# State pass, chunk scan, linear recurrence and gate projections: from a scheduled program to one hand-ordered list of 512 steps

## The chip, the core and the metric

The kernel runs on one core of a Trainium2 chip. The metric is the device time of one execution in microseconds (us). Three runs were timed, and one more execution was profiled; every row below comes from that one.

## What is computed

One layer of a backbone with a context prefix: three token mixers run in parallel on the modulated input, their outputs are gated and merged, then comes a mixture of experts. What matters here lies between the input projections and the merge.

```python
# Mamba-2 branch: chunks of 128 tokens, both directions d, heads in 4 groups
cb = jnp.einsum('bcqgn,bcsgn->bgcqs', cm, bm)
lmat = jnp.exp(_segsum(a))
y_diag = jnp.einsum('bgjcqs,bcsgjp->bcqgjp', cb[:, :, None] * lmat, xs)
st = jnp.einsum('bcsgn,bcsgjp->bcgjpn', bm, xs * decay_in[..., None])   # states
y_off = jnp.einsum('bcqgn,bcgjpn->bcqgjp', cm, entering) * decay_out[..., None]
y = y * jax.nn.silu(z)                                                  # then RMS norm, m2_w_out
# RG-LRU branch: two block projections, then a linear scan in each direction
r = sigmoid(xb @ lru_w_a + b);  ig = sigmoid(xb @ lru_w_x + b)
a_t = exp(-LRU_C * r * softplus(-lru_lam))
v = sqrt(max(-expm1(2.0 * log_a), EPS)) * (ig * xc32)
hd, fin = _linear_scan(a_t, v, h0)
# merge
g = sigmoid(gates)                                                      # 3 x 1024 columns of h @ w_in
merged = g0 * ya + g1 * yb + g2 * yc;  mx = merged @ w_o
x = x + mod_x[2] * mx     # mod = silu(c) @ w_mod + b_mod; mod_x[2] to mod_x[5] are first used after the merge
```

There are 1024 tokens and 256 context tokens, 1024 model columns, 16 heads in 4 groups, 10 chunks (8 of them with outputs), 512 recurrence columns.

## The kernel before, in words

**Precision.** A product of two fp32 matrices is made of three matmuls on rounded halves (high by high, high by low, low by high), 128x128 weights against 512 columns each: L265, L266 and L267 in mm3. ACT makes the high half of a weight block (L127) and VectorE (DVE) the low half (L128).

**The stage changed.** Between the input projections (pool p1) and the merge (pool p3b) stands pool p2. A scheduler orders its instructions on each engine, from their order in the program and their priorities. Its parts are:
- a head: softplus of dt, running sums of the log decay by three matmuls, and their rows, which go through device memory as rowsd (4 groups, 2 directions, 4 heads, 1024 tokens).
- states(): nine steps k with two directions each. An input block xk of 512 KB is loaded, GpSimd (POOL) scales it (L750, xd), PE makes four matmuls (L752, st), DVE carries the running state (L756, L762) and it is written back.
- chunk(g, c): 32 times. The decay rows arrive as rowb, broadcast to 128 partitions (L791); ACT takes the exponential of them (L796, dec); PE makes C*B (L798, pcb); DVE subtracts and bounds in eight instructions (L801); ACT takes the exponential (L802); GpSimd adds the directions (L803); DVE multiplies by pcb (L804); GpSimd scales dec (L805); PE makes eight matmuls into yps (L814, L815). After every fourth chunk come the gating by z and the sum of squares (L824 to L830).
- lru_tile(t): four times two directions. PE makes three lps products of three matmuls for each of two projections (L878), ACT makes tanh, exponentials and a root, DVE makes three element-wise instructions on 1283 columns (L885, L887, L888) and two scans (L890 to L895).
- z_task and gate_task: eight and 24 weight blocks, each 2 x 8 x 3 matmuls. Their matmuls (pj_z, pj_gt) are what PE can do while the chains above wait.
- mod_task(half): twice sixteen blocks of w_mod, 512 KB each, as moving operands of fp32 matmuls with one weight column (L912, pm); rows go to device memory as modd.

**The merge.** For each of eight blocks d of 128 columns, PE makes the products of the S5 and recurrence branches (bov, bog, bol), DVE merges them with the loaded gates, and the Mamba-2 output is scaled and split for the output product (L985, L994, tile ym). SyncE (SP) issues all large loads and stores in one queue, in program order.

In the rows, a matmul that isn't on rounded halves is shown as two records, so the four matmuls of a state product read x8. PEld is the loading of weights, which lies beside PE's matmuls.

## Time and profile before

| what | value |
|---|---|
| median of three runs | 2121.89 us (2120.39 to 2122.43) |
| profiled execution, its own time | 2120.92 us |
| its span, first to last instruction | 2119.14 us |
| mean granted TensorE clock, share of full | 0.956 |
| PE busy over the span | 1919.3 us (91%) |
| DVE busy | 1525.2 us (72%) |
| ACT busy | 1020.3 us (48%) |
| POOL busy | 510.4 us (24%) |
| state and scan stage (p2), by the trace | 523.5 to 1130 us |
| merge of the S5 and recurrence branches | 1130 to 1264 us |

The time of the profiled execution is 1.8 us above its span, which is what lies around the first and the last instruction. Busy shares are means over stages that are bound by different things, so the stage's own rows must be read.

### The profile page before, as it was taken

The numbers are of one execution on the slowest core, as the hardware profiler recorded it, in microseconds if no ns is written. First come the engines' busy times: TensorE is split into PE (matmuls) and PEld (weight loads), VectorE is DVE, ScalarE is ACT, GpSimd is POOL, SyncE is SP. The second block draws the span as 40 slices with busy tenths as digits, with TensorE's granted clock in tenths as the row PEclk, the third lists the DMA queues.
The fourth block names the chain that finished last, engine by engine and source line by source line (L and its number), as shares of the span: only waits on it lengthen the run. The fifth ranks groups of instructions, "written<-read, shape, count | busy, mean of one in ns | idle before, by whom it ended". The sixth has DMA issues, their size and how long they took to land.

```text
span 2119.1 us, 27213 instructions
## 1 busy us (share of the span) xinstructions
PE 1919.3 (91%) x9630; PEld 1516.2 (72%) x9630; DVE 1525.2 (72%) x2232; ACT 1020.3 (48%) x1313; POOL 510.4 (24%) x489
## 2 busy tenths in 40 slices
PE   5989999988889988879999999898299999999997
PEld 2678888877657666456577888687188888888885
DVE  4787788783454777667434655628899999999998
ACT  4434434432213665446332212222188888888785
POOL 1353333330142344233100000234501111100122
PEclk9999999999999999989999999999599999999999
DMA  8234334422586676777666554554599999999983
GB/s 313 54 81 114 101 95 117 122 90 90 180 261 192 186 212 175 242 180 210 208 174 188 180 160 153 186 200 149 196 339 381 400 389 404 387 389 393 391 312 137
DMA packets 301554, 462.67 MB, mean 218 GB/s; under 512 B 39945, under 2 KB 200121, under 8 KB 300393
## 3 DMA queue, kind: packets, MB, share of 16 engines
q1 hardware_dynamic: 297096, 445.19, 62.2%
q0 software_dynamic: 4320, 15.73, 2.9%
q8 instruction: 76, 1.25, 0.2%
q14 instruction: 62, 0.50, 0.1%
HBM read 384.44 MB, written 78.51 MB: 218 GB/s over the span
## 4 chain that ended last, share of the span: by engine, by line
PE 55%; DMA 9%; DVE 7%; issue 2%; ACT 1%; SPq 1%; POOL 1%; DVEq 0%; ACTq 0%; POOLq 0%
PE h_w L1443 6%; PE h_w L1445 6%; PE h_w L1444 6%; PE wo L1268 3%; DMA rowb<-rowsd 3%; PE py_w L1445 3%; PE py_w L1443 3%; PE py_w L1444 3%; PE pj_gt L267 2%; PE pj_gt L265 2%; PE pj_gt L266 2%; DMA wm<-in_w_mod_dram 2%; PE bom L266 1%; PE bom L265 1%; PE st L752 1%
## 5 line engine op out<-in xcount | busy, mean ns | idle before, releaser
L1338 DVE TENSOR_TENSOR el_w<-er_w,eh_w 128x1024 fp32r<-128x1024 f32 x384 | 460.7, 1220 | 25.0 <-ACT eh_w L1337 11.1
L1337 ACT CAST eh_w<-er_w 128x1024 fp32r<-128x1024 f32 x384 | 403.7, 1052 | 135.4 <-PE h_w L1444 58.9
L1443 PE MATMUL h_w<-eh_w,thi_x 128*128 128x512 f32 x512 | 202.9, 396 | 0.0
L1445 PE MATMUL h_w<-el_w,thi_x 128*128 128x512 f32 x512 | 200.2, 391 | 0.0
L1444 PE MATMUL h_w<-eh_w,tlo_x 128*128 128x512 f32 x512 | 199.8, 390 | 0.0
L801 DVE SCALAR_TENSOR_TENSOR rowb<-rowb,XL,lim 128x128 f32<-128x128 f32 x256 | 116.1, 518 | 72.1 <-ACT dec L796 72.1
L265 PE MATMUL pj_gt<-hxh,whi_gt 128*128 128x512 f32 x384 | 155.9, 406 | 11.9 <-ACT gz L779 11.9
L267 PE MATMUL pj_gt<-hxh,wlo_gt 128*128 128x512 f32 x384 | 155.3, 404 | 0.0
L266 PE MATMUL pj_gt<-hxl,whi_gt 128*128 128x512 f32 x384 | 155.1, 404 | 0.0
L1445 PEld LDWEIGHTS h_w<-el_w,thi_x 128*128 128x128 f32 x512 | 96.2, 188 | 20.4
L1444 PEld LDWEIGHTS h_w<-eh_w,tlo_x 128*128 128x128 f32 x512 | 96.5, 188 | 19.6 <-DVE tlo_x L1362 0.4
L1443 PEld LDWEIGHTS h_w<-eh_w,thi_x 128*128 128x128 f32 x512 | 96.5, 188 | 19.2 <-ACT thi_x L1361 0.2
L265 PEld LDWEIGHTS pj_gt<-hxh,whi_gt 128*128 128x128 f32 x384 | 74.4, 194 | 38.0 <-ACT gz L779 16.1
L1346 POOL DMA_INDIRECT xs<-h2d,idx x16 | 23.3, 1459 | 309.5 <-PE tb_x L1354 294.4
L1443 PE MATMUL py_w<-eh_w,thi_h 128*128 128x512 f32 x240 | 96.3, 401 | 0.0
L1445 PE MATMUL py_w<-el_w,thi_h 128*128 128x512 f32 x240 | 94.0, 392 | 0.0
L1444 PE MATMUL py_w<-eh_w,tlo_h 128*128 128x512 f32 x240 | 93.5, 390 | 0.0
L267 PEld LDWEIGHTS pj_gt<-hxh,wlo_gt 128*128 128x128 f32 x384 | 74.4, 194 | 25.4 <-issue 9.6
L266 PEld LDWEIGHTS pj_gt<-hxl,whi_gt 128*128 128x128 f32 x384 | 74.4, 194 | 20.5 <-issue 4.9
L796 ACT ACTIVATE dec<-rowb 64x512 f32<-64x512 f32 x64 | 40.2, 629 | 82.7 <-DMA rowb<-rowsd 72.7
L267 PE MATMUL pj_xb<-hxh,wlo_xb 128*128 128x512 f32 x192 | 76.8, 400 | 0.5 <-DVE wlo_xb L128 0.5
L265 PE MATMUL pj_xb<-hxh,whi_xb 128*128 128x512 f32 x192 | 76.7, 399 | 0.0
(653 smaller groups left out, 4894.7 us busy)
## 6 DMA issues: line engine op xcount, KB each, us to landing
er_w<-in_moe_w_dram SPq DMA_DIRECT2D x384, 512.0 KB
...
```

The source lines that it names most:

```text
L265: T.matmul(ps, wh(k), xh(k), start=(first and k == 0), stop=False)
L266: T.matmul(ps, wh(k), xl(k), start=False, stop=False)
L267: T.matmul(ps, wl(k), xh(k), start=False, stop=(last and k == nk - 1))
L796: A.activation(dec[64 * d:64 * d + 64], rowb[64 * d:64 * d + 64, d], AF.Exp)
L801: V.scalar_tensor_tensor(rowb[:, d, h], rowb[:, d, h], XL[:, c, d, 4 * g + h:4 * g + h + 1], lim[:, d], op0=ALU.subtract, op1=ALU.min)
L1268: T.matmul(st4[i]["ps"][n], ms[i][a][:, k], wo[k][b][:, sl], start=(k == 0 and q == 0), stop=(k == KC - 1 and q == 2))
L1337: A.copy(a, raw)
L1338: V.tensor_sub(b, raw, a.bitcast(F32))
L1346: G.indirect_dma_start(out=xsb[e], out_offset=None, in_=h2d[:, :], in_offset=bass.IndirectOffsetOnAxis(ap=idx[:, e:e + 1], axis=0))
L1443: T.matmul(ps[n], xa[:, j, :], a[:, sl], start=(j == 0), stop=False)
L1444: T.matmul(ps[n], xb[:, j, :], a[:, sl], start=False, stop=False)
L1445: T.matmul(ps[n], xa[:, j, :], b[:, sl], start=False, stop=(j == KC - 1))
```

## The change

The stage is written out as one list of 512 steps under a manual order for DVE, ACT and PE: weight block w (32 of them: eight of z, 24 of gates), column half c and contraction block k. Each step makes the three matmuls of one gate block (L1091 of the new program). All other work is hung on steps by plan(step, function): states from step 22 with 5 steps for each k, chunks from step 54 with 12.4 steps each, recurrence rounds from step 81 with 45 steps for each direction. At one step the planned functions run first, then the gate matmuls, and each engine executes its own instructions in that order. SP is not in the manual order.

GpSimd's element-wise work in the stage (L750, L803, L805, L830 and the recurrence splits L860, L865) moves to DVE. The eight L801 become two instructions on 128x1024. rowsd is laid out by chunk, so the broadcast load reads 4 KB in one piece for each partition instead of eight of 512 bytes. The buffers of rowb, xe and bc go from three to four, and xk borrows two more. The stage has a PSUM pool of its own, with two banks each for gates, pcb, yps (shared with st) and lps. The softplus of dt and the constants of the recurrence move to the end of p1. The modulation leaves PE and the stage: the merge loads the same 32 blocks of w_mod, multiplies and adds them on DVE (four and 28 instructions on 128x1024), and sums over partitions with eight matmuls; the tiles of ym share 16 buffers with these blocks.

```diff
+ST0, STP = 22, 5
+CH0, CHP = 54, 12.4
+LR0, LRP = 81, 45
+MEN3 = {mybir.EngineType.DVE, mybir.EngineType.Activation, mybir.EngineType.PE}
...
+            if hb == 7:
+                softplus(dt, 320, p1, "d")
+                lru_consts()
...
-    rowsd = dr.tile([4, 2, 4, S], F32, name="rowsd")
+    rowsd = dr.tile([4, 8, 2, 4, P], F32, name="rowsd")
...
+    ps2 = tc.alloc_tile_pool(name="ps2", bufs=1, space=PSUM, reuse_waits="tile")
+    pb2 = lambda tag, nm: ps2.tile([P, 512], F32, tag=tag, name=nm, bufs=2)
+    with tc.tile_pool(name="p2", bufs=1, reuse_waits="tile") as p2, tc.manual_schedule(engines=MEN3):
+
+        steps = [(w, c, k) for w in range(32) for c in range(2) for k in range(KC)]
...
+        def plan(at, f, *args):
+            todo.setdefault(max(int(at), 0), []).append((f, args))
+
+        def w_load(w):
+            col = OFF_Z + w * P if w < 8 else OFF_G + (w - 8) * P
+            raws[w] = wp.tile([P, KC, P], F32, tag="raw", name=f"raw_zg{w}", bufs=3)
+            Y.dma_start(raws[w], dap(I["w_in"], col, [[7200, P], [P * 7200, KC], [1, P]]))
...
+        def z_tanh(w, c):
+            zts[w, c] = zp.tile([P, 512], F32, tag="zt", name=f"zt{w}{c}", bufs=3)
+            A.activation(zts[w, c], pps[w, c], AF.Tanh, scale=0.5)
+            if w >= 8:
+                Y.dma_start(gtd[(w - 8) // KC][(w - 8) % KC][:, c * 512:(c + 1) * 512], zts[w, c])
...
+        for w in range(32):
+            plan(16 * w - 40, w_load, w)
+            plan(16 * w - 13, w_hi, w)
+            plan(16 * w - 10, w_lo, w)
+            for c in range(2):
+                plan(16 * w + 8 * c + 9, z_tanh, w, c)
+                if w < 8:
+                    plan(16 * w + 8 * c + 11, z_mul, w, c)
...
-                    G.tensor_mul(v16(xd), v16(xk[:, 0:D]), dtd[:, c, d, :, None].to_broadcast([P, 16, 64]))
...
+        def st_load(k, d):
+            c = (cf, cb)[d](k)
+            tag = ("xk", "xk", "xk", "lxc", "lq")[(2 * k + d) % 5]
+            xk = xks[k, d] = p2.tile([P, 1283], F32, tag=tag, name=f"xk{k}{d}", bufs=3 if tag == "xk" else 1)
+            Y.dma_start(xk[:, 0:D].rearrange("p (g e) -> p g e", g=4), xed[c][:, :, 0:256])
+            Y.dma_start(xk[:, D:D + 256], btd[c])
+
+        def st_mul(k, d):
+            c = (cf, cb)[d](k)
+            xds[k, d] = p2.tile([P, D], F32, tag="xd", name=f"xd{k}{d}", bufs=2)
+            V.tensor_mul(v16(xds[k, d]), v16(xks[k, d][:, 0:D]), dtd[:, c, d, :, None].to_broadcast([P, 16, 64]))
...
+        for k in range(9):
+            o = ST0 + STP * k
             for d in range(2):
...
+                plan(o - 22, st_load, k, d)
+                plan(o + 2 * d, st_mul, k, d)
+                plan(o + 4 + 2 * d, st_mm, k, d)
+            plan(o + 3, st_dec, k)
+            plan(o + 8, st_add, k)
...
-            Y.dma_start(rowb.rearrange("p d h q -> p (d h) q"), dap(rowsd, g * 8 * S + q0, [[0, P], [S, 8], [1, P]]))
...
             for d in range(2):
-                for h in range(4):
-                    V.scalar_tensor_tensor(rowb[:, d, h], rowb[:, d, h], XL[:, c, d, 4 * g + h:4 * g + h + 1], lim[:, d], op0=ALU.subtract, op1=ALU.min)
-            A.activation(rowb, rowb, AF.Exp)
-            G.tensor_add(rowb[:, 0], rowb[:, 0], rowb[:, 1])
-            V.tensor_mul(rowb[:, 0], rowb[:, 0], pcb[:, None, 0:P].to_broadcast([P, 4, P]))
-            G.tensor_mul(dec, dec, Cd[:, None, :].to_broadcast([P, 4, P]))
...
+        def c_load(i):
+            g, c = gc[i]
+            bcs[i] = p2.tile([P, 2, P], F32, tag="bc", name=f"bc{i}", bufs=4)
+            Y.dma_start(bcs[i], bcd[g][:, :, c * P:(c + 1) * P])
+            rows_[i] = p2.tile([P, 2, 4, P], F32, tag="rowb", name=f"rowb{i}", bufs=4)
+            Y.dma_start(rows_[i].rearrange("p d h q -> p (d h q)"), dap(rowsd, (8 * g + c) * 8 * P, [[0, P], [1, 8 * P]]))
...
+            V.tensor_sub(rowb, rowb, XL[:, c, :, 4 * g:4 * g + 4][:, :, :, None].to_broadcast(sh))
+            V.tensor_tensor(rowb, rowb, lim[:, :, None, :].to_broadcast(sh), op=ALU.min)
...
+        def c_dec(i):
+            V.tensor_mul(decs[i], decs[i], bcs[i][:, 1, :][:, None, :].to_broadcast([P, 4, P]))
+
+        def c_mul(i):
+            rowb = rows_[i]
+            V.tensor_add(rowb[:, 0], rowb[:, 0], rowb[:, 1])
+            V.tensor_mul(rowb[:, 0], rowb[:, 0], pcbs[i][:, None, 0:P].to_broadcast([P, 4, P]))
...
+        for i in range(32):
+            o = CH0 + CHP * i
+            plan(o - 2.5 * CHP, c_load, i)
+            plan(max(o - 2.5 * CHP, ST0 + STP * max(gc[i][1] + 1, 8 - gc[i][1]) + 8.5), c_xe, i)
+            plan(o, c_args, i)
+            plan(o + 1, c_cb, i)
+            plan(o + 7, c_exp, i)
+            plan(o + 8, c_dec, i)
+            plan(o + 11, c_mul, i)
+            plan(o + 17, c_mm, i, 0)
+            plan(o + 18, c_mm, i, 1)
+            if i % 4 == 3:
+                j = i // 4
+                plan(o - CHP, q_load, j)
                 for t in range(2):
...
+                    plan(o + 20 + t, q_out, j, t)
+                    plan(o + 22 + t, q_gate, j, t)
+                    plan(o + 25 + t, q_sq, j, t)
+                    plan(o + 28 + t, q_sum, j, t)
...
+        for t in range(4):
+            o = LR0 + 2 * LRP * t
+            plan(o - 18, l_load, t)
+            plan(o - 9, l_cast, t)
+            for d in range(2):
+                for e in range(2):
+                    for b in range(3):
+                        plan(o + 9 * e + 3 * b, l_mm, t, d, e, b)
+                        plan(o + 9 * e + 3 * b + 2, l_act, t, d, e, b)
+                plan(o + 21, l_exp, t, d)
+                plan(o + 28, l_q, t, d)
+                plan(o + 31, l_sqrt, t, d)
+                plan(o + 35, l_in, t, d)
+                plan(o + 37, l_scan, t, d)
+                o += LRP
+            plan(o, l_out, t)
...
-        def mod_task(half):
-            pm = psp.tile([P, 512], F32, tag="pm", name=f"pm2_{half}", bufs=1)
-            for j in range(KC):
-                for q in range(2):
-                    wm = p2.tile([P, 1024], F32, tag="wm2", name=f"wm{half}{j}{q}", bufs=2)
-                    Y.dma_start(wm, dap(I["w_mod"], j * 6 * D + 2 * D + half * 2 * D + q * D, [[KC * 6 * D, P], [1, 1024]]))
-                    for n in range(2):
-                        r = 32 * (2 * q + n)
-                        T.matmul(pm[r:r + 1, :], scc[:, j, 0:1], wm[:, n * 512:(n + 1) * 512], start=(j == 0), stop=(j == KC - 1))
...
+        for n, (w, c, k) in enumerate(steps):
+            for f, args in todo.pop(n, []):
+                f(*args)
+            if k == 0:
+                pps[w, c] = pb2("pp", f"pj_zg{w}{c}")
+            hi, lo = ws[w]
+            sl = slice(c * 512, (c + 1) * 512)
+            for o, (a, b) in enumerate(((hi, hxh), (hi, hxl), (lo, hxh))):
+                T.matmul(pps[w, c], a[:, k, :], b[k][:, sl], start=(k == 0 and o == 0), stop=(k == KC - 1 and o == 2))
...
-        ym = [(p3b.tile([P, S], F32R, name=f"yhi_m{k}"), p3b.tile([P, S], F32R, name=f"ylo_m{k}")) for k in range(8)]
+        ym = []
...
+        def mod_part(q, j):
+            wm = p3b.tile([P, D], F32, tag="ym", name=f"wm{q}{j}", bufs=16)
+            Y.dma_start(wm, dap(I["w_mod"], j * 6 * D + 2 * D + q * D, [[KC * 6 * D, P], [1, D]]))
+            if j == 0:
+                mq[q] = wm
+                V.tensor_scalar(wm, wm, scc[:, j, 0:1], None, op0=ALU.mult)
+                return
+            V.scalar_tensor_tensor(mq[q], wm, scc[:, j, 0:1], mq[q], op0=ALU.mult, op1=ALU.add)
+            if j < KC - 1:
+                return
+            pm = psp.tile([P, 512], F32, tag="pm", name=f"pm2_{q}", bufs=1)
+            for n in range(2):
+                T.matmul(pm[32 * n:32 * n + 1, :], ones[:, 0:1], mq[q][:, n * 512:(n + 1) * 512], start=True, stop=True)
...
+                for _ in range((5, 5, 5, 5, 4, 4, 4, 0)[d]):
+                    mod_part(*mparts.pop(0))
+                ym.append(tuple(p3b.tile([P, S], F32R, tag="ym", name=f"y{e}_m{d}", bufs=16) for e in ("hi", "lo")))
                 load_y(ym[d], m2_dram[d // 2][:, d % 2, :], f"m{d}", m2h[:, d:d + 1])
```

**Order on PE in the states.** Before, around one step k of the states (pj_z are the z products, st the state products of the two directions):

```order
L266 MATMUL pj_z_512_5267<-hxl_380,whi_z_5234 128x512
L752 MATMUL st_0_4594<-xd_4599,xk_4596 64x256 x2
L752 MATMUL st_1_4595<-xd_4599,xk_4596 64x256 x2
L267 MATMUL pj_z_512_5267<-hxh_372,wlo_z_5235 128x512
L265 MATMUL pj_z_512_5267<-hxh_373,whi_z_5234 128x512
L266 MATMUL pj_z_512_5267<-hxl_381,whi_z_5234 128x512
L267 MATMUL pj_z_512_5267<-hxh_373,wlo_z_5235 128x512
L265 MATMUL pj_z_0_5558<-hxh_366,whi_z_5554 128x512
L266 MATMUL pj_z_0_5558<-hxl_374,whi_z_5554 128x512
L752 MATMUL st_0_4594<-xd_4608,xk_4605 64x256 x2
L752 MATMUL st_1_4595<-xd_4608,xk_4605 64x256 x2
```

After, around the same kind of place (pj_zg are z and gate products alike):

```order
L1091 MATMUL pj_zg_4730<-hxl_375,whi_zg_4575 128x512
L1091 MATMUL pj_zg_4730<-hxh_367,wlo_zg_4576 128x512
L836 MATMUL st_0_4746<-xd_4714,xk_4553 64x256 x2
L836 MATMUL st_1_4747<-xd_4714,xk_4553 64x256 x2
L1091 MATMUL pj_zg_4730<-hxh_368,whi_zg_4575 128x512
L1091 MATMUL pj_zg_4730<-hxl_376,whi_zg_4575 128x512
L1091 MATMUL pj_zg_4730<-hxh_368,wlo_zg_4576 128x512
L1091 MATMUL pj_zg_4730<-hxh_369,whi_zg_4575 128x512
L1091 MATMUL pj_zg_4730<-hxl_377,whi_zg_4575 128x512
L1091 MATMUL pj_zg_4730<-hxh_369,wlo_zg_4576 128x512
L836 MATMUL st_0_4746<-xd_4728,xk_4556 64x256 x2
L836 MATMUL st_1_4747<-xd_4728,xk_4556 64x256 x2
```

The two directions' state products stay four matmuls each; what stood between them by the scheduler's choice is now a fixed two steps of three gate matmuls.

**Order on DVE in a recurrence round.** Before, late in the chunks (rowb is a chunk's decay block, lq, li and la are recurrence tiles, xq the gated output):

```order
L801 SCALAR_TENSOR_TENSOR rowb_5838<-rowb_5838,XL,lim 128x128 x4
L801 SCALAR_TENSOR_TENSOR rowb_5884<-rowb_5884,XL,lim 128x128 x8
L804 TENSOR_TENSOR rowb_5838<-rowb_5838,pcb_5843 128x512
L885 SCALAR_TENSOR_TENSOR lq_5912<-lq_5912,lr_5815 128x1283
L128 TENSOR_TENSOR wlo_gt_7479<-raw_gt_7476,whi_gt_7478 128x1024
L804 TENSOR_TENSOR rowb_5884<-rowb_5884,pcb_5889 128x512
L801 SCALAR_TENSOR_TENSOR rowb_5930<-rowb_5930,XL,lim 128x128 x8
L887 SCALAR_TENSOR_TENSOR li_5816<-li_5816,lxc_5483 128x1283
L888 SCALAR_TENSOR_TENSOR li_5816<-lq_5912,li_5816 128x1283
L804 TENSOR_TENSOR rowb_5930<-rowb_5930,pcb_5935 128x512
L894 SCALAR_TENSOR_TENSOR lq_5912<-la_5911,li_5816 128x256
```

After, in the second direction of the first recurrence tile (dec, lwl, lxl and lxe were written by GpSimd before):

```order
L1019 SCALAR_TENSOR_TENSOR li_5570<-li_5570,lxc_5086 128x1283
L926 SCALAR_TENSOR_TENSOR xq_5590<-xq_5590,Dc,yps_5528 128x512
L926 SCALAR_TENSOR_TENSOR xq_5590<-xq_5590,Dc,yps_5539 128x512
L900 TENSOR_TENSOR dec_5774<-dec_5774,bc_5547 128x512
L1026 SCALAR_TENSOR_TENSOR li_5570<-lq_5742,li_5570 128x1283
L930 TENSOR_TENSOR xq_5590<-xq_5590,zq_5591 128x512
L984 TENSOR_TENSOR lwl_5844<-lw_5779,lwh_5843 128x512
L989 TENSOR_TENSOR lxl_5848<-lxc_5781,lxh_5847 128x1024
L989 TENSOR_TENSOR lxe_5849<-lxc_5781,lxe_5849 128x256
L930 TENSOR_TENSOR xq_5590<-xq_5590,zq_5591 128x512
L1035 SCALAR_TENSOR_TENSOR lq_5742<-la_5741,li_5570 128x256
L1036 SCALAR_TENSOR_TENSOR lq_5742<-la_5741,lq_5742,li_5570 128x1024
```

The round's long instructions stand in one run with the four-chunk output, the next tile's splits and a dec product, and no decay block stands between them.

**Order on DVE in the merge.** Before (sgf, s and mgs are merge halves, yr_m the Mamba-2 output, ylo_m its low half):

```order
L1030 SCALAR_TENSOR_TENSOR sgf<-sgf,bov_8656 128x512
L1031 SCALAR_TENSOR_TENSOR sgf<-gtf,sgf 128x512
L1032 SCALAR_TENSOR_TENSOR s_8695<-gtf,bol_8658 128x512
L1033 SCALAR_TENSOR_TENSOR mgs_8653<-sgf,s_8695 128x512
L985 SCALAR_TENSOR_TENSOR yr_m_8751<-yr_m_8751,m2h,rbc_8591 128x1024
L1030 SCALAR_TENSOR_TENSOR s_8743<-s_8743,bov_8704 128x512
L1031 SCALAR_TENSOR_TENSOR s_8743<-gt_8701,s_8743 128x512
L994 TENSOR_TENSOR ylo_m_8576<-yr_m_8751,yhi_m_8575 128x1024
L1032 SCALAR_TENSOR_TENSOR s_8744<-gt_8701,bol_8706 128x512
```

After, at the same block:

```order
L1209 SCALAR_TENSOR_TENSOR mgs_8300<-sgf,s_8342 128x512
L1171 TENSOR_SCALAR wm_8398<-wm_8398,scc 128x1024
L1206 SCALAR_TENSOR_TENSOR s_8390<-s_8390,bov_8351 128x512
L1173 SCALAR_TENSOR_TENSOR wm_8398<-wm_8401,scc,wm_8398 128x1024
L1207 SCALAR_TENSOR_TENSOR s_8390<-gt_8348,s_8390 128x512
L1173 SCALAR_TENSOR_TENSOR wm_8398<-wm_8404,scc,wm_8398 128x1024
L1208 SCALAR_TENSOR_TENSOR s_8391<-gt_8348,bol_8353 128x512
L1173 SCALAR_TENSOR_TENSOR wm_8398<-wm_8407,scc,wm_8398 128x1024
L1125 TENSOR_TENSOR wlo_s_8563<-raw_s_8562,whi_s_8561 128x1536
L1209 SCALAR_TENSOR_TENSOR mgs_8300<-s_8390,s_8391 128x512
L1173 SCALAR_TENSOR_TENSOR wm_8398<-wm_8410,scc,wm_8398 128x1024
L1137 SCALAR_TENSOR_TENSOR yr_m_8415<-yr_m_8415,m2h,rbc_8238 128x1024
```

Between the four merge instructions of each half now stand the products of w_mod blocks, ahead of the scaling of yr_m.

## Rows read from the trace of the kernel before

**Rows 1.** Windows: us; busy of PE, PEld, DVE, ACT, POOL; clock; DMA share; GB/s.
```profile
523.50:604.00 80.50, 64.93 (x268) 46.98 (x267) 37.02 (x82) 22.36 (x36) 22.18 (x14) 0.89 0.65 200
604.00:664.00 60.00, 60.00 (x252) 39.52 (x251) 29.00 (x29) 7.47 (x10) 22.03 (x13) 1.00 0.75 236
664.00:1036.00 372.00, 317.79 (x1641) 229.63 (x1639) 253.61 (x371) 205.35 (x261) 129.36 (x98) 0.93 0.70 198
1036.00:1130.00 94.00, 91.62 (x408) 67.57 (x408) 32.19 (x38) 30.09 (x32) 5.05 (x3) 1.00 0.60 183
1130.00:1264.00 134.00, 134.00 (x576) 107.65 (x575) 73.87 (x88) 28.10 (x33) 0.00 (x0) 1.00 0.57 179
1650.00:1700.00 50.00, 50.00 (x234) 41.67 (x233) 47.94 (x48) 40.19 (x43) 5.41 (x3) 1.00 1.03 401
```

**Rows 2.** Chain of waits in 664 to 1036: start us, us, what.
```profile
767.12 11.44 DMA rowb<-rowsd
866.00 0.96 PE pm L912 x4
```

**Rows 3.** Waits in 664 to 1036: us in total, times, longest us.
```profile
DVE rowb L801 <- ACT dec L796: 57.5, 17, 7.6
ACT dec L796 <- DMA rowb<-rowsd: 55.2, 12, 11.2
PE pm L912 <- DMA wm<-in_w_mod_dram: 15.7, 4, 5.9
```

**Rows 4.** PE timeline, gates alone: start us, us, engine, line, operation.
```profile
1080.04 0.39 PE L266 MATMUL pj_gt<-hxl,whi_gt 128*128 128x512 f32 x1
...
1089.56 0.39 PE L266 MATMUL pj_gt<-hxl,whi_gt 128*128 128x512 f32 x1
```

**Rows 5.** PE timeline around one state product.
```profile
643.52 0.39 PE L265 MATMUL pj_z<-hxh,whi_z 128*128 128x512 f32 x1
643.84 1.94 PE L752 MATMUL st<-xd,xk 128*64 128x256 f32 x8
645.71 0.50 PE L266 MATMUL pj_z<-hxl,whi_z 128*128 128x512 f32 x1
```

**Rows 6.** PE timeline around one C*B product.
```profile
979.84 0.39 PE L266 MATMUL pj_gt<-hxl,whi_gt 128*128 128x512 f32 x1
980.16 0.48 PE L798 MATMUL pcb<-bc 64*128 64x128 f32 x2
980.58 0.50 PE L267 MATMUL pj_gt<-hxh,wlo_gt 128*128 128x512 f32 x1
```

**Rows 7.** PE timeline around one chunk output.
```profile
984.79 0.39 PE L267 MATMUL pj_gt<-hxh,wlo_gt 128*128 128x512 f32 x1
985.11 0.45 PE L814 MATMUL yps<-rowb,xe 128*64 128x128 f32 x4
...
986.18 0.50 PE L265 MATMUL pj_gt<-hxh,whi_gt 128*128 128x512 f32 x1
```

**Rows 8.** PE timeline around one recurrence product.
```profile
799.39 0.40 PE L267 MATMUL pj_gt<-hxh,wlo_gt 128*128 128x512 f32 x1
...
800.33 0.40 PE L265 MATMUL pj_gt<-hxh,whi_gt 128*128 128x512 f32 x1
```

**Rows 9.** Groups on DVE, 523 to 1060: busy us, mean ns, idle before.
```profile
L801 DVE SCALAR_TENSOR_TENSOR rowb<-rowb,XL,lim 128x128 f32<-128x128 f32 x256 | 116.1, 518 | 72.1 <-ACT dec L796 72.1
L804 DVE TENSOR_TENSOR rowb<-rowb,pcb 128x512 f32<-128x512 f32 x32 | 21.7, 677 | 18.8 <-PE pcb L798 13.4 <-POOL rowb L803 5.3
L895 DVE TENSOR_TENSOR_SCAN lq<-la,lq,li 128x1024 f32<-128x1024 f32 x4 | 9.4, 2342 | 0.1
```

**Rows 10.** Line L888 alone: ns min/median/max.
```profile
L888 DVE SCALAR_TENSOR_TENSOR li<-lq,li x8: 1480/2460/2584, 702.8 to 1026.2; 128x1283 f32<-128x1283 f32 x8
```

**Rows 11.** Groups on DVE in the merge, 1130 to 1264.
```profile
L985 DVE SCALAR_TENSOR_TENSOR yr_m<-yr_m,m2h,rbc 128x1024 f32<-128x1024 f32 x8 | 10.3, 1284 | 41.2 <-DMA yr_m<-m_dram 41.2
```

**Rows 12.** Groups on POOL, 523 to 1060.
```profile
L750 POOL TENSOR_TENSOR xd<-xk,dtd 128x1024 f32<-128x1024 f32 x18 | 36.4, 2026 | 47.2 <-DMA xk<-xed 21.1 <-PE st L752 15.8 <-DVE dtd L718 7.0
```

More of the change, by code (lines that the diff above doesn't have):

```diff
@@ L833, in backbone @@
[L833 to L845 removed]
+        v16 = lambda t: t.rearrange("p (h e) -> p h e", h=16)
@@ new lines, in q_gate, with q_sq, q_sum @@
+        def q_gate(j, t):
+            xq, zq = quad[j]
+            V.tensor_mul(xq[:, t], xq[:, t], zq[:, t])
+            if t == 1:
+                Y.dma_start(m2_dram[j // 2][:, :, (j % 2) * 512:(j % 2 + 1) * 512], xq)
+        def q_sq(j, t):
+            xq, zq = quad[j]
+            first = j < 2 and t == 0
+            A.activation(ssum[:, j % 2 * 512:(j % 2 + 1) * 512] if first else zq[:, t], xq[:, t], AF.Square, scale=0.5)
+        def q_sum(j, t):
+            sl = slice(j % 2 * 512, (j % 2 + 1) * 512)
+            if not (j < 2 and t == 0):
+                V.tensor_add(ssum[:, sl], ssum[:, sl], quad[j][1][:, t])
@@ L934, in backbone @@
[L934 to L944 removed]
+            (t0, n, h_, l_) = ((0, 512, xh_[:, 0:512], xl_[:, 0:512]), (512, 512, xh_[:, 512:S], xl_[:, 512:S]), (1027, SC, xe_[:, 0], xe_[:, 1]))[b]
@@ L945, in backbone @@
+        for n in sorted(todo):
+            for f, args in todo[n]:
+                f(*args)
+    ps2.release()
+    psp = psstack.enter_context(tc.tile_pool(name="psp", bufs=1, space=PSUM, reuse_waits="tile"))
     if dbg is not None:
```

431 lines of the change are left out of this document (216 added, 215 removed).

## Prediction

> **What bounds the kernel now.** I read the windows first, since the mean over the span hides the stages [rows 1]. The changed stage runs from 523.5 to 1130 us, 606.5 us in four windows. PE is busy in 64.9, 60.0, 317.8 and 91.6 us of them, 534.3 in all, while DVE sums to 351.8, ACT to 265.3 and POOL to 178.6. So 72 us pass with PE idle, and its busy time is stretched too: the granted clock is 0.89 in the first window and 0.93 in the third, against 1.00 where PE is never idle (604 to 664). From 1036 to 1130, where the gates run nearly alone, PE is busy in 91.6 of 94 us.
>
> Then the chain of waits and the list of waits, to see what PE idles for. In the third window a rowb load lies on the chain with 11.44 us [rows 2], the first decay exponential waits 55.2 us for such loads, DVE waits 57.5 us for that exponential (largely the same time, handed on), and PE waits 15.7 us for w_mod blocks [rows 3]. The stage is thus a sequence of dependent pieces across five engines with PE as its fullest engine, not a stage in which one engine is full. If the waits go, PE's own work is the floor.
>
> **The floor on PE.** 1536 gate matmuls: in the stretch of gates alone 42 matmuls lie between the two starts of the timeline, 9.52 us, so 0.2267 us each [rows 4], 348.2 us. Each other product is priced by what it adds to the distance of two gate matmuls. The new order says how often PE changes over to each:
> - A state product of four matmuls: 645.71 - 643.52 less 0.23 is 1.96 us [rows 5]; 18 of them, 35.3 us.
> - C*B: 0.74 less 0.23 is 0.51 [rows 6]; 32 of them, 16.3.
> - Chunk output: all eight matmuls took 1.39 less 0.23, 1.16 us [rows 7]. The list splits them in two with a gate step between. Half is 0.58; a second change-over can cost no more than the whole lone C*B product, 0.51, half of which lies on each half, so 0.58 to 0.83. I take 0.70: 64 of them, 44.8 (37 to 53).
> - Recurrence: 0.94 less 0.23 is 0.71 for a product of 512 columns [rows 8]; 32 of these and 16 of 256 columns at half, 28.5.
> - Sums, transposes, norm: some 4 us.
>
> Together 477.1 us. The 64 modulation matmuls, 0.96 us for two [rows 2], some 31 us with their waits on top, are no longer here.
>
> **Is another engine's sum larger?** For DVE, take off L801's 116.1 [rows 9] and add 64 instructions of 1024 columns at 1.28, as L985 took with GpSimd at rest [rows 11], 82; 18 state scalings at 1.28, 23, which GpSimd made in 2.03 [rows 12]; 78 of 512 columns at 0.68 as L804 [rows 9], 53; and the recurrence splits, 9. That gives 403 us, with the other instructions at the means that they had while GpSimd worked. ACT's work stays, 265. Both are under 477, so neither bounds the stage as a whole. The Trainium skill (Perfetto Trace Analysis, Optimizing Scalar/DVE Operations) says that with DVE saturated it may pay to hand work to Scalar or even GpSimd; this change does the reverse. If DVE were the bound in its fullest stretches, the time would be that of rival 1.
>
> **Waits that remain.** The manual order lets no gate step forward over a late piece, so slack must be read from the step numbers; a step is 0.68 us of gates.
> - States: a state product, two gate steps, the other, and the next step's first product five steps after this one's. DVE must scale the next block (1.28) and add two halves (2 x 0.68) in the gap of PSUM reuse, 2.64 against the three gate steps before the next product, 2.04. With queue effects about 0.9 us on each of nine, 8 in all (0 to 20).
> - Recurrence rounds: the twelve DVE rows shown are two of 1283 columns at L888's quick 1.48 [rows 10], the scan at 2.34 [rows 9], a split at 1.28, six of 512 columns at 0.68, a split and a scan of 256 at about 0.4 and 0.8: 11.9 us, planned within eleven steps that hold about 10 us of PE. The dec and rowb products behind the run have six steps (4.1 us and what PE does between) before PE needs them. I charge 1.5 us in each of eight rounds: 12 (0 to 26).
> - Rowb loads: asked for 2.5 chunks, 31 steps or over 21 us ahead; the slow landing was 11.44 [rows 2]. Hidden; without that cover each chunk would pay the 11 us less what the other rowb buffers give.
> - The head: the softplus goes to the end of the previous stage and the gates run from step 0 beside the rest. 3 us (0 to 6) for the first weights.
> - To the merge: the last recurrence splits stand behind the last gate's tanh on ACT. 4 (0 to 12).
>
> Stage: 477.1 + 8 + 12 + 3 + 4 = 504.1 us, 102 less than 606.5.
>
> **The merge.** It took 134 us with PE full at clock 1.00, DVE busy for 73.9 and the DMA share at 0.57 [rows 1]. Added: 32 DVE instructions of 1024 columns at 1.28 [rows 11], 41, and small adds, so DVE comes to some 118 of 139 us. The 32 loads are 16.8 MB; at the 401 GB/s of a stretch where the DMA share was 1.03 [rows 1] that is 42 us of all engines, so the share goes from 76 of 134 to about 119 of 139. On PE come eight matmuls at 0.48, 4 us, with their change-over 5. For waits 5 (0 to 25): 144 us.
>
> **The sum.** Before: 606.5 + 134 = 740.5. After: 504.1 + 144 = 648.1. Saved 92.4. The profiled execution's own time was 2120.92, so 2028.5; the median of the runs shown is 1.0 higher, so 2029.
>
> GpSimd's absence may give DVE more: L888 took 1.48 us at the least and 2.46 in the median of its eight, while GpSimd was at work nearby [rows 10]. I have used the quick price in the rounds, because GpSimd has no element-wise work left there. With the median a round's three instructions of that length are 3 us longer, 8 x 3 = 24 us more, and the rounds' term goes from 12 up to 36. The Trainium skill (SBUF — State Buffer, Who interferes with whom) states that a DVE instruction with two SBUF inputs contends with a GpSimd instruction that reads SBUF; by it the term stays at 12, and the two prices of L888 agree with it so far as one line can.
>
> **Rivals.**
> 1. VectorE becomes the bound in the recurrence rounds. For it: its sum rises from 352 to at most 403 in a stage that shrinks to 504, so 80% of it, and its work comes in runs. The sixteen steps from 160 hold the last eleven rows of the run shown (10.4 us), two rowb products (1.4), a decay block (2.6), a weight split (1.3), two sums (1.4), a dec product (0.7) and the recurrence's output (2.6), 20.4 us in all, against 10.9 of gates and 3.4 of other products on PE. Against it: 100 us of room, and the pieces are spread over 45 steps. If each of the eight rounds stops PE by that excess, 6.1 us, it is 49 in place of 12: 2066. PE's clock, which fell to 0.93 where PE idled [rows 1], would come in here as well.
> 2. The merge pays for the modulation. Its gate loads stand in SP's queue behind blocks of w_mod that wait for a free buffer, and the scaling of yr_m behind their products on DVE; the output product needs all of ym. The 25 us bound of the merge's waits in place of 5: 2049. For it: yr_m already made DVE wait 41.2 us for loads [rows 11], off PE's path. Against it: PE stayed full through that.
> 3. Slower than before. In the old order PE filled a late chunk with whatever gate was ready; now a rowb that is late stops all 32 chunks on PE. This decides if a chunk waits 92.4 / 32 = 2.9 us; then the time is 2121 and above it slower. For it: rowb waits of up to 11.2 us [rows 3]. Against: 21 us of lead, and the load no longer comes in 512-byte pieces.
>
> **Chances and range.** Forecast (2006 to 2046) 0.60; faster still, if waits and change-overs are near their low ends, 0.04; rival 1 0.18; rival 2 0.13; rival 3 0.05. From 2004 to 2070 the range takes in the forecast, rival 2 and rival 1 up to a little over its worked-out value, and leaves out rival 3, the upper part of rival 1 and the fastest cases, under 0.2. Within 0.2% of before, about what a measurement of this kernel can tell from no change: 0.01, the point where rival 3 just cancels the gain; slower 0.05; faster 0.94.
>
> **What would show it.** Right: the stage some 505 us long, PE busy over 94% of it at clock 0.98 or more, gates still at 0.227 apart, no rowb load on the chain of waits, L888's successor near 1.5 us throughout, and a merge of about 144 us. Rival 1: PE waits for rowb or dec products behind DVE scans in each round, and a lower clock. Rival 2: the merge over 155 us, with PE waiting for ym or gate tiles. Rival 3: ACT's first exponential waiting for rowb in most chunks. The prediction is wrong if the stage stays above 560 us, or if the time before 523.5 or after the merge moves by more than some 5 us.

## The result, and the profile after

| | median us | range | ratio to the kernel before |
|---|---|---|---|
| before | 2122.14 | 2120.39 to 2122.43 | |
| after | 2051.95 | 2051.04 to 2054.53 | 0.9673 [0.9656, 0.9690] |

The change saved 70 us, the forecast said 93 (2029, range 2004 to 2070). The profiled execution has a span of 2049.3 us against 2119.1. The windows of the changed kernel, from the first gate step to the start of the output product, answer to [rows 1] (same columns):

```profile
522.40:540.00 17.60, 16.87 (x78) 13.32 (x77) 8.39 (x17) 9.54 (x15) 0.00 (x0) 1.00 0.21 66
540.00:580.00 40.00, 29.39 (x113) 18.35 (x112) 18.34 (x20) 2.73 (x4) 0.00 (x0) 0.83 0.97 310
580.00:720.00 140.00, 137.97 (x660) 95.98 (x659) 98.46 (x110) 61.94 (x80) 1.55 (x7) 1.00 0.67 206
720.00:740.00 20.00, 14.27 (x66) 10.41 (x65) 16.47 (x18) 10.41 (x16) 0.10 (x1) 0.83 0.69 221
740.00:1044.40 304.40, 301.05 (x1523) 226.12 (x1521) 199.40 (x213) 174.73 (x216) 4.10 (x12) 0.99 0.58 179
1044.40:1064.00 19.60, 11.02 (x28) 7.66 (x29) 12.22 (x9) 7.62 (x8) 0.00 (x0) 0.65 0.70 217
1064.00:1195.40 131.40, 131.40 (x567) 103.06 (x566) 109.85 (x131) 26.20 (x29) 0.00 (x0) 1.00 0.86 300
```

From the list's start to 1044.4 us are 522.0 us, where the forecast had 500.1 (504.1 less the 4 for the transition), and from there to the output product 151.0, where it had 148. So against the forecast the list lost 22 us and the merge 3; some 2 us came back outside them. The clock tells where to look: it is 0.83 in 540 to 580, 0.83 in 720 to 740 and 0.65 at the entry to the merge, and 0.99 to 1.00 elsewhere. PE's waits in the same stretch name the three places (line, what for, us in total, times, longest us), and answer to [rows 3]:

```profile
PE st L836 <- issue: 12.1, 2, 10.6
PE yps L914 <- issue: 7.8, 2, 5.7
PE bol L268 <- ACT yhi_l L1145: 5.7, 1, 5.7
PE bog L270 <- DVE wlo_f L1125: 2.1, 1, 2.1
PE lps L1001 <- DVE lxl L989: 0.9, 1, 0.9
```

One wait of 10.6 us stands before a state product, one of 5.7 before a chunk's output, one of 5.7 at the first recurrence product of the merge. No w_mod block and no rowb load is in the list. On DVE the eight L801 of a chunk became two instructions of 1.22 us (L889, L890); L905 is the old L804 [rows 9]:

```profile
L889 DVE TENSOR_TENSOR rowb<-rowb,XL 128x1024 f32<-128x1024 f32 x32 | 39.1, 1222 | 49.2 <-ACT dec L888 36.1 <-DMA raw_zg<-in_w_in_dram 4.8 <-DMA bc<-bcd 4.2
L905 DVE TENSOR_TENSOR rowb<-rowb,pcb 128x512 f32<-128x512 f32 x32 | 22.0, 687 | 2.3
```

The old L888, which had 2.46 us in the median [rows 10], is now L1026, and quick in all eight:

```profile
L1026 DVE SCALAR_TENSOR_TENSOR li<-lq,li x8: 1485/1487/1496, 675.6 to 982.1; 128x1283 f32<-128x1283 f32 x8
```

### The profile page after: what moved, and what is told of

Read it like the earlier page. It is cut to its first block, busy times and chain, and to the rows that moved or that the text cites. A ratio compares the mean times of both kernels' runs of the same rounds, so it can differ in the third digit from the quotient of the medians.

```text
span 2049.3 us, 26714 instructions
## 1 busy us (share of the span) xinstructions
PE 1892.8 (92%) x9518; PEld 1500.2 (73%) x9518; DVE 1576.0 (77%) x2180; ACT 1025.2 (50%) x1315; POOL 338.2 (17%) x381
## 4 chain that ended last, share of the span: by engine, by line
PE 58%; DVE 6%; issue 1%; DMA 1%; ACT 1%; POOL 1%; SPq 0%; DVEq 0%; ACTq 0%
PE pj_zg L1091 12%; PE h_w L1624 6%; PE h_w L1622 6%; PE h_w L1623 6%; PE wo L1447 3%; PE py_w L1624 3%; PE py_w L1622 3%; PE py_w L1623 3%; PE lps L1001 1%; PE bom L269 1%; PE bom L270 1%; PE bom L268 1%; PE yps L914 1%; DVE tu L1288 1%; PE bog L270 1%
## 5 line engine op out<-in xcount | busy, mean ns | idle before, releaser
L1091 PE MATMUL pj_zg<-hxh,whi_zg 128*128 128x512 f32 x512 | 212.8, 416 | 0.7 <-DVE zt L736 0.6
L1091 PE MATMUL pj_zg<-hxh,wlo_zg 128*128 128x512 f32 x512 | 200.9, 392 | 0.0
L1091 PE MATMUL pj_zg<-hxl,whi_zg 128*128 128x512 f32 x512 | 200.9, 392 | 0.0
L1091 PEld LDWEIGHTS pj_zg<-hxh,whi_zg 128*128 128x128 f32 x512 | 96.5, 188 | 38.5 <-issue 16.3
L730 ACT ACTIVATE zt<-pj_zg 128x512 f32<-128x512 f32 x64 | 38.3, 599 | 163.4 <-PE pj_zg L1091 157.2
L1091 PEld LDWEIGHTS pj_zg<-hxh,wlo_zg 128*128 128x128 f32 x512 | 96.5, 188 | 21.7
L1091 PEld LDWEIGHTS pj_zg<-hxl,whi_zg 128*128 128x128 f32 x512 | 96.8, 189 | 16.2
L889 DVE TENSOR_TENSOR rowb<-rowb,XL 128x1024 f32<-128x1024 f32 x32 | 39.1, 1222 | 49.2 <-ACT dec L888 36.1
L269 PE MATMUL pj_xb<-hxl,whi_xb 128*128 128x512 f32 x192 | 76.4, 398 | 0.0
```

The lines of the kernel that those rows point to most:

```text
L269: T.matmul(ps, wh(k), xl(k), start=False, stop=False)
L730: A.activation(zts[w, c], pps[w, c], AF.Tanh, scale=0.5)
L889: V.tensor_sub(rowb, rowb, XL[:, c, :, 4 * g:4 * g + 4][:, :, :, None].to_broadcast(sh))
L1091: T.matmul(pps[w, c], a[:, k, :], b[k][:, sl], start=(k == 0 and o == 0), stop=(k == KC - 1 and o == 2))
```

## The experiments

All times are medians of five runs; the ratio is to runs of the kernel before on the same chip, whose medians are 2122 to 2126 us. Runs on different chips are compared by ratio, so a difference by ratio can be up to 5 us apart from that by medians.

**1. A buffer of its own for rw.** The first suspect for the 10.6 us: DVE waited 7.7 us for rw's stores. rw now shares its buffer with ssum, which takes it from step 60.

```diff
-        rw = p2.tile([32, S], F32, tag="Sn", name="rw", bufs=2)
+        rw = p2.tile([32, S], F32, tag="ss", name="rw", bufs=1)
```

> The tile rw (the decay rows on their way out) no longer shares its buffers with the running state Sn; it shares with ssum, which is used much later. Theory A: in the changed kernel PE's 10.6 us wait before the third state product is the xk block of that step, asked for late because SP's queue holds early loads for the chunks ahead of it; then nothing changes, 2052 us within 2, and PE waits 8 to 11 us there again. Rival B: the running state Sn waits for rw's eight stores (DVE sat idle 7.7 us until they had landed), so the wait falls by about 8 us and the clock loss after it goes too: 2038 to 2044 us.

Measured 2049.7 us, ratio 0.9650 [0.9629, 0.9671], an interval that overlaps the changed kernel's; PE's wait was 10.7 us. DVE no longer waits for rw's stores, and waits the longer for the xk block:

```profile
DVE xd L830 <- DMA xk<-xed: 13.2, 2, 12.7
```

Theory A stands, with the time 0.3 us outside its 2 us: the buffer isn't what held PE.

**2. No early loads at the head.** SP's timeline in the changed kernel (start us, us, operation, count) shows what stood ahead of the third step's second xk block:

```profile
552.13 5.21 SPq L803 DMA_DIRECT2D rowsd<-rw  x8
...
559.51 0.57 SPq L823 DMA_DIRECT2D xk<-xed  x1
```

Eight small stores take SP 5.2 us, and from 541.8 us on they stood behind ten loads for later work (C and B blocks, weights, a gating block); the xk block is asked for at 559.5. DVE scales it ahead of adding the second step's states, which frees the banks that PE waits for.

```diff
+            if i < 4:
+                V.memset(bcs[i][:, 0, 0:1], 0.0)
+                V.memset(rows_[i][:, 0, 0, 0:1], 0.0)
...
+            if j == 0:
+                V.memset(xq[:, 0, 0:1], 0.0)
+                V.memset(zq[:, 0, 0:1], 0.0)
...
-            G.memset(lw, 0.0)
+            (G if t else V).memset(lw, 0.0)
```

> The loads of the first four chunks, of the first gating block and of the first recurrence weights can't be issued before their own steps of the list, since DVE first writes one element into each of their tiles. Theory A (SP's queue and what it loads early): PE's wait of 10.6 us at the third state product goes below 3 us, and the 13.65 us at half clock behind it, some 7 us of work, go with it: 2035 us, 2033 to 2042. Rival C: the DMA engines themselves are full there (share 0.97 from 540 to 580 us), so the blocks land late in any order: above 2047 us.

Measured 2049.3 us, 0.9638 [0.9616, 0.9661], an interval that overlaps the changed kernel's. The wait fell from 10.6 to 4.6 us, the stage by 3, and the 15 us expected did not come. The window of the head, and what DVE waits for in it:

```profile
540.00:580.00 40.00, 35.36 (x139) 22.40 (x138) 23.25 (x29) 3.41 (x5) 0.00 (x0) 0.91 0.98 304
```
```profile
DVE xd L829 <- DMA xk<-xed: 6.2, 2, 5.7
DVE Sn L842 <- DMA rowsd<-rw: 1.5, 1, 1.5
```

The rowsd stores no longer hold Sn up (1.5 us for 7.7), but an xk block is still waited for 5.7 us with the DMA share at 0.98. So both were half right: the queue's order was worth 6 us of PE's wait. That the rest is the DMA engines being full is argued from their share; no run shows it.

**3. Chunk products at one step.**

```diff
-            plan(o + 1, c_cb, i)
+            plan(o + 6, c_cb, i)
...
-            plan(o + 17, c_mm, i, 0)
-            plan(o + 18, c_mm, i, 1)
+            plan(o + 18.4, c_mm, i, 0)
+            plan(o + 18.4, c_mm, i, 1)
```

> Each chunk's C*B product and both halves of its output stand at one step of the list (with the neighbouring chunk's), in place of three: 64 change-overs between gates and other products fewer. Theory A: a change-over costs 0.09 us before the inserted product and 0.11 us on the gate after it, which the forecast left out, so 64 x 0.20 = 13 us less: 2039 us, 2036 to 2044. Rival: the gates' longer starts are no cost of the change-over but waits that go elsewhere; then 2052 us within 3.

Measured 2042.1 us, 0.9608 [0.9587, 0.9629]: 10 us less by the medians, 14 by ratio, and the list 11 us shorter. Recurrence products have the gates' own form and cost nothing extra (last section), so a change-over is one from these two to another product. The trace has 56 of them in place of 119, 63 fewer: 63 x 0.20 = 12.6, theory A. The window of the list in the changed kernel and in this one:

```profile
522.40:1044.20 521.80, 499.56 (x2432) 364.18 (x2430) 340.91 (x375) 259.15 (x330) 5.75 (x20) 0.98 0.63 194
```
```profile
524.50:1034.90 510.40, 483.99 (x2432) 372.18 (x2430) 340.57 (x375) 258.86 (x329) 5.75 (x20) 0.98 0.64 199
```

PE is busy for 15.6 us less and waits 4 us more, so 0.20 is rather low for some of them. The timeline of the changed kernel around half an output, and of this one around the end of a whole one with its C*B:

```profile
741.82 0.39 PE L1091 MATMUL pj_zg<-hxh,wlo_zg 128*128 128x512 f32 x1
742.14 0.45 PE L914 MATMUL yps<-rowb,xe 128*64 128x128 f32 x4
742.41 0.40 PE L915 MATMUL yps<-dec,xe 128*64 128x128 f32 x4
742.74 0.50 PE L1091 MATMUL pj_zg<-hxh,whi_zg 128*128 128x512 f32 x1
743.08 0.40 PE L1091 MATMUL pj_zg<-hxl,whi_zg 128*128 128x512 f32 x1
```

```profile
744.79 0.40 PE L1091 MATMUL pj_zg<-hxh,wlo_zg 128*128 128x512 f32 x1
...
746.19 0.49 PE L894 MATMUL pcb<-bc 64*128 64x128 f32 x2
746.61 0.50 PE L1091 MATMUL pj_zg<-hxh,whi_zg 128*128 128x512 f32 x1
746.95 0.40 PE L1091 MATMUL pj_zg<-hxl,whi_zg 128*128 128x512 f32 x1
```

In the first, 742.74 - 741.82 less 0.23 is 0.69, the 0.70 of the forecast; but the gate that starts at 742.74 holds PE until 743.08, 0.34 in place of 0.23. That 0.11 is paid after each such product. Ahead of a C*B product alone stand 0.09 us ([rows 6]: 0.32 in place of 0.23), so one change-over fewer saves 0.20 there. Two halves of an output take 2 x (0.69 + 0.11) = 1.60 us and a whole one 1.16 + 0.11 = 1.27 ([rows 7]), so there it saves 0.33. 32 x 0.33 and 31 x 0.20 are 16.8, near the 15.6.

**4. The old layout of the rows.** rowsd and its stores are as before too; the load is shown.

```diff
-            Y.dma_start(rows_[i].rearrange("p d h q -> p (d h q)"), dap(rowsd, (8 * g + c) * 8 * P, [[0, P], [1, 8 * P]]))
+            Y.dma_start(rows_[i].rearrange("p d h q -> p (d h) q"), dap(rowsd, g * 8 * S + c * P, [[0, P], [S, 8], [1, P]]))
```

> The decay rows are laid out as before, so each rowb load reads eight pieces of 512 bytes for each partition. Theory A (the forecast): the loads are asked for 31 steps ahead and slow ones of some 11 us are hidden, so 2052 us within 3 in spite of them. Rival: the slower loads hold the DMA engines longer and the first chunks and states wait for them: 2060 us or more, with ACT's first exponential waiting for rowb.

Measured 2087.9 us, 0.9826 [0.9803, 0.9849], 36 us more. The rival's time is right and its place in part: ACT's first exponential doesn't wait for rowb, but states and other loads are late. PE's waits for states rise from 12.1 to 25.4 us, for outputs from 7.8 to 23.1, for recurrence products from 0.9 to 4.5, some 32 us together. Waits of the changed kernel, then of this one:

```profile
DVE xd L829 <- DMA xk<-xed: 6.0, 2, 5.5
ACT lxh L988 <- DMA lxc<-xcd: 6.3, 2, 3.4
```

```profile
DVE xd L828 <- DMA xk<-xed: 24.8, 4, 14.0
ACT lxh L987 <- DMA lxc<-xcd: 24.2, 3, 9.6
```

From 640 to 1000 us the DMA engines are busy for 0.69 with 178 GB/s here, against 0.60 with 185 (below), and move 64.0 MB in 77611 packets against 66.8 in 54011. Fewer bytes in more packets hold the engines longer, and the xk and lxc blocks, planned 22 and 18 steps ahead and not 31 as rowb, are late.

**5. The recurrence splits five steps later.**

```diff
-            plan(o - 9, l_cast, t)
+            plan(o - 4, l_cast, t)
```

> The split of a recurrence tile's input and weights stands 4 steps ahead of its first product instead of 9, some 4.5 us later. Theory A: PE's waits of 5.7 and 2.1 us for a chunk's output at the changes of recurrence tile come from the input block lxc, which has one buffer and lands some 2.8 us too late; ACT and DVE stand still for it in their fixed order, and the rowb products behind wait too. Then these waits fall below 1 us each and the half clock after them (6.8 and 3.4 us long) goes: 12 us less, 2040 us, 2036 to 2046. Rival B, the forecast's: it is DVE's sum in these runs of 12 us; then the waits stay above 4 and 1.5 us, and the time at 2052 within 3.

Measured 2057.8 us, 0.9693 [0.9674, 0.9711], an interval that overlaps the changed kernel's: not faster. The times of both fell. The waits moved:

```profile
PE lps L1001 <- DVE lxl L989: 7.1, 2, 4.4
PE yps L914 <- issue: 2.9, 2, 2.0
```

Outputs wait 2.9 us in place of 7.8 and recurrence products 7.1 in place of 0.9; the sum, 10.0 us, is above the 8.7 before. ACT waits for no lxc block any more (6.3 us before). At the first change of tile the output's wait goes from 5.7 to 0.9: DVE no longer stands 2.7 us for the late block ahead of the output's rowb products, and the splits, 2.3 us, come behind them. At the second it is 2.0 for 2.1. But the later split is now late itself, 2.6 and 4.4 us, behind the other instructions of the run. So a late load and DVE's run both count, and what an lxc block in time would give with the split in its old place was not tried.

**6. The same program, ordered by the scheduler.**

```diff
-    with tc.tile_pool(name="p2", bufs=1, reuse_waits="tile") as p2, tc.manual_schedule(engines=MEN3):
+    with tc.tile_pool(name="p2", bufs=1, reuse_waits="tile") as p2:
```

> The same program text as the changed kernel, list of steps, engines, rows and merge included, but the stage's instructions are ordered by the scheduler again and not by hand. Theory A (the hand order took the waits away): the stage goes back towards 560 us or more, 2085 us, 2070 to 2115. Rival: the gain is from the moved work, the rows and the modulation, whatever the order; then 2065 us or less.

Measured 2013.2 us, 0.9469 [0.9452, 0.9485]: 39 us faster than the changed kernel by the medians, 43 by ratio, and on the far side of even the rival. PE's waits up to the output product:

```profile
PE bog L268 <- ACT zt L730: 8.4, 1, 8.4
PE pj_zg L1091 <- DVE zt L736: 3.8, 2, 2.7
PE st L836 <- DVE xd L829: 1.5, 1, 1.5
```

Within the stage PE waits for 6 us, against 22 under the hand order, and the granted clock is 1.00 over all of it. The gates end 482 us after the first one, where the list takes 522. The head shows one reason. The first state product of the third step, in the changed kernel and then here:

```profile
569.53 3.64 PE L836 MATMUL st<-xd,xk 128*64 128x256 f32 x8 [10.62 <-issue]
```
```profile
568.45 1.08 PE L836 MATMUL st<-xd,xk 128*64 128x256 f32 x4
```

It starts scarcely sooner, but from the second step's last product to it PE makes gates with 1.1 us of waiting, where the fixed order lets none pass and PE stands for 10.6 us.

**7. The modulation alone, in the kernel before.** mod_part and the shared buffers of ym as in the change, mod_task's two calls left out, nothing else.

> The kernel before, with one part of the change alone: the modulation is taken off PE and the stage, and made by DVE in the merge. Theory A: the stage loses 31 us of PE work and the 16 us of waits for w_mod blocks in it, the merge pays some 8 us for the eight small matmuls and its waits, so 39 us less: 2083 us, 2074 to 2093. Rival: the waits for w_mod stood beside the chunks' own waits, and only PE's work counts, 31 less 8 us: 2099 us, 2094 to 2104.

Measured 2101.1 us, 0.9894 [0.9876, 0.9913], 1.06% or 22 us: the rival, as PE's work without the waits. PE's idle time in the stage stays, 74 us for 72.

**8. Two chunk instructions back on GpSimd, in the list.** GpSimd joins the manual order.

```diff
-MEN3 = {mybir.EngineType.DVE, mybir.EngineType.Activation, mybir.EngineType.PE}
+MEN3 = {mybir.EngineType.Pool, mybir.EngineType.DVE, mybir.EngineType.Activation, mybir.EngineType.PE}
...
-            V.tensor_mul(decs[i], decs[i], bcs[i][:, 1, :][:, None, :].to_broadcast([P, 4, P]))
+            G.tensor_mul(decs[i], decs[i], bcs[i][:, 1, :][:, None, :].to_broadcast([P, 4, P]))
...
-            V.tensor_add(rowb[:, 0], rowb[:, 0], rowb[:, 1])
+            G.tensor_add(rowb[:, 0], rowb[:, 0], rowb[:, 1])
```

> In the list, two of the moved instructions of each chunk (adding the directions of the decay block, and scaling dec) go back to GpSimd, at the same steps. Theory A: GpSimd takes 1.3 to 1.5 us for what DVE makes in 0.68, and DVE's two-input instructions beside it go from 1.2 to 1.7 us and more, so the chunks' chain is later by 1.4 us and more and PE waits in many chunks: 2060 us, 2054 to 2085. Rival: DVE is relieved of 43 us, and slack takes the rest up: 2050 us or less.

Measured 2053.5 us, 0.9657 [0.9639, 0.9675], no difference from the changed kernel: between the two forecasts. The price of GpSimd's neighbourhood shows all the same. The second of L801's two new instructions, the same in both programs and at the same step, in the changed kernel and then here:

```profile
L890 DVE TENSOR_TENSOR rowb<-rowb,lim x32: 1224/1225/1227, 602.5 to 990.9; 128x1024 f32<-128x1024 f32 x32
```
```profile
L890 DVE TENSOR_TENSOR rowb<-rowb,lim x32: 1224/2189/2210, 601.5 to 994.6; 128x1024 f32<-128x1024 f32 x32
```

GpSimd took over 64 instructions of 0.68 us, 44 us of DVE's work, and DVE is busy for 339.8 us in the list, against 340.9: what is left on it grew by as much. So DVE was not relieved, as the rival had it, and the chunks' steps had the slack for the slower instructions, against theory A.

**9. Modulation and rows in the kernel before; 10. and DVE in place of GpSimd.** Number 9 adds the new rowsd and its loads to number 7; number 10 also writes V for G in states, chunk and lru_tile and takes the two instructions for L801. The old program text, buffers and scheduler stay.

> The kernel before with two parts of the change: the modulation in the merge (alone it gave 25 us) and the contiguous decay rows (taken out of the changed kernel they cost 36 us). Theory A: the rows are worth as much here, where rowb loads stood on the chain of waits: 2101 - 36 = 2065 us, 2055 to 2075. Rival: here the scheduler lets gates fill the waits for rowb, so the rows give little: 2092 to 2102 us.

> As the kernel with contiguous rows and the moved modulation, and also GpSimd's element-wise work of the stage on DVE and two instructions in place of L801's eight. Theory A: the chunk's chain loses GpSimd's instructions of 1.3 to 1.5 us and the quarrel with DVE, so the stage gains another 25 us or more over the one without this part, to 2025 to 2045 us. Rival: DVE has no time to spare in the old order (it already made 352 us of work) and the gain is under 8 us; what is left to 2013 us is then from the list's own program order and its deeper buffers.

Measured 2060.6 us, 0.9688 [0.9673, 0.9703], and 2012.7 us, 0.9467 [0.9453, 0.9481]. Theory A held in both; in the second the gain was 48 us, larger than expected, and the time below the range given.

**11. Number 6 with the old rows; 12. number 6 with all of GpSimd's work given back to it.** In number 12 the two instructions in place of L801's eight stay.

> The changed program under the scheduler, with the decay rows laid out as before. Theory A: the slower rowb loads cost what they cost under the hand order, 36 us: 2049 us, 2040 to 2060. Rival: a scheduler's order and four buffers hide them: 2013 to 2022 us, with PE's waits below 15 us in the stage; the 36 us would then be the price of the fixed order only.

> The changed program under the scheduler, with all of the stage's element-wise work that the change took from GpSimd given back to it. Theory A: GpSimd's slower instructions and its quarrel with DVE make the chunks' chain late, and PE waits again: 2035 us, 2025 to 2060. Rival: PE is the bound with slack to spare and nothing is seen: 2010 to 2018 us.

Measured 2049.5 us, 0.9653 [0.9637, 0.9670], and 2049.1 us, 0.9642 [0.9628, 0.9657]: theory A's time in both. In number 11 PE waits 27 us in the stage for 6, and ACT 36.1 us for lxc blocks, as in number 4. In number 12 PE waits 22 us, but little of it, 4.7, for chunk outputs. The longest wait is a gate in the head, for a z product that is late on DVE; ahead of it three of DVE's instructions on 1024 columns take 2.3 to 2.9 us beside GpSimd in place of 1.22. L1026, too, is slow again in half of its eight:

```profile
PE pj_zg L1091 <- DVE zt L736: 14.8, 2, 12.9
```
```profile
L1026 DVE SCALAR_TENSOR_TENSOR li<-lq,li x8: 1480/1976/2581, 687.8 to 966.3; 128x1283 f32<-128x1283 f32 x8
```

One row of the windows, 640 to 1000 us, sums the series up (columns of [rows 1]). In turn: before, number 7, number 9, number 10, the changed kernel, number 6, number 4.

```profile
640.00:1000.00 360.00, 310.06 (x1588) 224.81 (x1587) 243.05 (x355) 189.57 (x243) 130.34 (x99) 0.94 0.71 197
```
```profile
640.00:1000.00 360.00, 305.24 (x1548) 232.44 (x1547) 248.00 (x360) 193.58 (x250) 131.07 (x101) 0.92 0.68 182
```
```profile
640.00:1000.00 360.00, 326.70 (x1727) 251.08 (x1726) 266.71 (x382) 212.68 (x272) 140.27 (x105) 0.97 0.60 190
```
```profile
640.00:1000.00 360.00, 357.83 (x1934) 283.67 (x1933) 261.99 (x290) 224.35 (x287) 4.21 (x18) 1.00 0.64 202
```
```profile
640.00:1000.00 360.00, 351.17 (x1788) 260.46 (x1785) 258.42 (x277) 217.31 (x275) 2.46 (x16) 0.99 0.60 185
```
```profile
640.00:1000.00 360.00, 360.00 (x1892) 279.85 (x1890) 260.90 (x285) 227.21 (x286) 4.13 (x17) 1.00 0.63 197
```
```profile
640.00:1000.00 360.00, 331.64 (x1680) 244.83 (x1678) 240.45 (x262) 203.12 (x261) 2.98 (x17) 0.97 0.69 178
```

PE busy goes 310, 305, 327, 358 as the three parts come in, with the scheduler's order all the way; the hand order has 351 and the scheduler on the same program 360, all of the window. The window is the same stretch of time, not of work: the faster programs are further on in it.

## Why the prediction came out right, point by point

The time lay in the range, 23 us above the value given. It lay above the 2006 to 2046 that the forecast itself was given; the range reached 2070 for rivals 1 and 2, and neither came. So the hit owes something to luck. The view that PE's own work is the floor was right: in number 6 PE is busy without a break from 640 to 1000 us. What the terms were:

- **The floor, 477.1 us, was too low by 13.** The step "each other product is priced by what it adds to the distance of two gate matmuls" stopped one matmul short. The gate after a state, C*B or output product takes 0.34 in place of 0.23, 114 x 0.11 = 12.5 us. It could be read in the kernel before: in [rows 7] the gate after the output starts at 986.18, and the next one 0.34 later:

```profile
986.52 0.39 PE L266 MATMUL pj_gt<-hxl,whi_gt 128*128 128x512 f32 x1
```

Number 3 bears the price out.
- **The waits, 23 us, were right in sum (12.1 + 7.8 + 0.9 in the rows above and 1.5 of small ones, 22.3) and wrong in place, so that the sum agrees is luck.** The states were given 0.9 us each; one of them took 10.6, for a load. The step on the rowb loads ("Hidden") named the right load as safe, but didn't ask which loads SP issues early; number 2 shows 6 of the 10.6 us to be theirs.
- **The clock was left out of the sum.** A granted clock of 0.83 in 40 and in 20 us, and 0.99 in 304, is some 24 us at the lower of the two levels, half of full, so up to 12 us of matmuls. It was in rival 1's text only. 13 + 12 less 1 for the waits is 24; the list missed by 22, so the other products were priced some 2 us too high or the clock cost less than 12.
- **The recurrence rounds, 12 us, were right in size:** 8.7 us of PE waits, though in three places and not in each of eight rounds. In the longest, 5.7 us, DVE stood 2.7 us for a late lxc block (number 5), a load that the term did not have; that DVE's run makes the rest is argued. Rival 1's 49 us did not come. DVE's sum, the ground for that rival, was put at up to 403 us and came to 341, less than the 352 before, with GpSimd's work on top. Some of it left the stage with the softplus and the modulation; for the rest, the prediction left DVE's other instructions at their means beside GpSimd.
- **The price of DVE without GpSimd was right:** 1.49 us in L1026. What the forecast did not see is that the work moved off GpSimd is one of the three causes of the gain. It booked that work as more load on DVE, with a maybe on the prices. Numbers 8 and 12 have the other side: 2.19 us for 1.22 in L890, 1.98 for 1.49 in L1026, in the median beside GpSimd. By the Trainium skill (SBUF — State Buffer, Who interferes with whom), two-input DVE instructions contend with GpSimd's reads; these traces agree. The Trainium skill (Perfetto Trace Analysis, Optimizing Scalar/DVE Operations) ties its advice to hand work to GpSimd to a saturated DVE, and adds that moving work between these two might not help. That condition is missing here, with all the work on DVE and it busy for 262 of 360 us (number 10), and number 8 agrees with the addition.
- **The merge, 144 us and 4 for the entry, took 151:** 8.6 us of idle PE at the entry, where the clock was 0.65; inside, PE is busy throughout with the DMA share at 0.86. Rival 2 did not come.
- **"The manual order lets no gate step forward over a late piece"** was written as a cost to be estimated, but the forecast priced the change as a whole and did not ask what each part gives, and this is the one part of it that loses. By ratios, in points of 2122 us: modulation 1.06 (22 us), rows 2.06 (44), DVE for GpSimd with L801's two instructions 2.21 (47); together 5.33, and number 6, which has the list's text, own PSUM pool and deeper buffers besides, is not apart from number 10 (0.9469 and 0.9467). The hand order gives back 2.04 (43). Rows and GpSimd taken back one at a time from number 6 give 1.84 and 1.73, so the parts add up fairly. Number 12 keeps L801's two instructions, so the work moved is worth 1.73 by itself in that program, and some half a point is left for the two instructions.

Where they go can be counted in the two traces, whose lists differ by 39 us: 16 us more of waits (22 against 6), up to 12 us of clock, 34 more change-overs (119 against 85) at 0.20, 7 us, and 9 us by state products side by side (below). That is 32 to 44; how much the clock cost was not shown by itself. Not tried: a hand order with later states and grouped products together; L801's two instructions alone.

Numbers 6 and 10 beat both kernels, each by 2.1% over the changed one (0.9469 and 0.9467 over 0.9673). Number 10 needs no list at all.
